# Half of the first modulation on TensorE, one pair's down blocks later, the mixer's gate and loads moved

## The chip, the core and the metric

The kernel runs on one core of a Trainium2 chip. Its time is the device time of one execution in microseconds (us); a kernel's time is the median over its runs. The core has five engines that run side by side and wait for each other by semaphores: PE (TensorE, matmuls; PEld is its weight load), DVE (VectorE), ACT (ScalarE), POOL (GpSimd) and SP (SyncE, which here only issues DMAs). Each engine works through its own list of instructions in order. A DMA that waits for a free buffer therefore holds every DMA behind it in the same list.

## The reference, cut to what matters

One layer of an encoder: x is 1024 rows of 1024 numbers, and three sublayers change it one after the other. `silu(c) @ w_ada + b_ada` gives nine vectors of 1024: a shift, a scale and a gate for each sublayer.

```python
mod = (silu(c) @ w_ada + b_ada).reshape(b, 3, 3, D_MODEL)

def sublayer(h, i, fn, resid_w):
    shift, scale, gate = mod[:, i, 0], mod[:, i, 1], mod[:, i, 2]
    u = rms_norm(h, norm_pre[i]) * (1.0 + scale) + shift
    return h + resid_w * gate * rms_norm(fn(u), norm_post[i])

h = sublayer(h, 0, lambda u: (silu(u @ wg1) * (u @ wu1)) @ wd1, 0.5)
h = sublayer(h, 1, token_mixer, 1.0)
h = sublayer(h, 2, lambda u: (silu(u @ wg2) * (u @ wu2)) @ wd2, 0.5)
```

The hidden width of the two feed-forward networks (FFN) is 2816. The mixer in between projects u to queries, keys, values and two gates, runs two kinds of attention, merges their results by the gates and projects once more. Everything is 32-bit.

## The kernel before, in words

**Matmuls.** Every operand of a large product is split into two fp32r halves, H (a cast on ScalarE) and L (the rest, a subtraction on VectorE), and each product of two tiles is three matmuls: H times H, L times H, H times L. A tile is 128 partitions by 512 columns.

**The FFN, first phase (gate/up).** `ffn` (line 477) runs over eleven pairs of hidden blocks; a pair c has a gate matrix and an up matrix (`Matrix`, line 301). Products of two-by-two blocks are made with seven block products instead of eight (Strassen-Winograd). `start` makes the two products that need plain weights (24 matmuls). `rest` (line 414) makes the other five: `sums` loads the weight blocks again (lines 325 and 327) and forms S2 and S1 on VectorE (lines 330 and 331), `sums34` and `last` make S3, S4 and A22, and then `p6`, `p5`, `p7`, `p3`, `p4` are twelve matmuls each (lines 297 to 299). For the first three pairs (`NFIRST`) `start` has been run ahead of the loop, so only `rest` is left for them.

**Between the two phases.** When a pair is done, `hidden` (line 437) forms the block sums of its result on VectorE (lines 443 to 446) and stores them to DRAM, and `down_sums` (line 462) loads the pair's down weights (lines 465 and 467), forms their sums (lines 470 to 473) and stores them too. For pair 0 both stand at the end of its turn in the loop, in front of pair 1. For a later pair c, `down_sums` stands between its two matrices.

**The FFN, second phase (down).** Seven products p = 0 to 6, each over the eleven pairs: a pair's two blocks are loaded (line 542, tile `stg`, six buffers), split (lines 224 and 225) and multiplied into four PSUM banks, A or B (lines 547 to 549). Product 4 goes on in bank B, whose content after product 3 is first copied out (line 599). The tile `grow` (the sublayer's gate row, line 536) is loaded at the start and used by `finish`. After the last products come post-norm, residual and the next pre-norm.

**The modulation.** Factors that are needed later are formed in small steps by generators. A step is one 512 KB load (line 87) and one multiply-add on VectorE (lines 89 and 91). `mod_col` (lines 97 to 104) turns a vector into columns with eight one-column matmuls (line 101); `mod_gate` makes a gate row in ten steps, with two fp32 matmuls (line 125), loads of the bias and norm rows (lines 119 and 121) and a store (line 130). The gate/up phase takes `per_pair` steps after each pair (3 in the first FFN, 1 in the second), the down phase takes one step at each place in `STEPS`. In the first FFN the gate/up phase makes gate 0 and the factors of sublayer 1 (30 steps), and the down phase makes gate 1 (the mixer's) and the factors of sublayer 2 (30 steps). In the second FFN the gate/up phase makes gate 2 (10 steps).

**The start.** The factors of sublayer 0 are made in `start0_` in four column blocks `cb` of 512 columns, each from four loads of 512 KB (line 654) into eight buffers. VectorE sums eight products into `m0` (lines 658 and 660), and four one-column matmuls against `ones` (line 675) add up the partitions. Lines 679 to 681 finish the factors of two of the eight k-tiles. The transposes of x (line 186), the modulation (lines 177 to 180) and parts of the first `start` products follow, block by block.

**The mixer.** Its first three jobs (queries, keys, values; four weight loads, line 137, into two buffers) are called when the first FFN has been written down in the program.

**Order.** The program is written in one order; a planner at build time then puts each engine's list in order, and may bring an instruction forward where it reckons that its engine is free. `keep_in_program_order` and `issue_after` pin an instruction behind another one.

Of the kernel before, what the change touches and what calls it, by code (L numbers as in the profile page):

```python
# [16 lines left out]
ALU = mybir.AluOpType  # L17
# [21 lines left out]
STEPS = ((0, 2, 4, 6, 8), (0, 2, 4, 6, 8), (2, 4, 6, 8, 10), (2, 6), (0, 4, 8), (4, 6, 8, 9, 10))  # L39
# [7 lines left out]
def build(ctx, tc, A, out):  # L47
# [84 lines left out]
    ab, gates = {}, {}  # L132

# [280 lines left out]
    def rest(late, ms, again):  # L414
# [15 lines left out]
        m.last()  # L430
        m.p6()
# [45 lines left out]
    def ffn(wg, wu, wd, start, pending, steps_fn, per_pair, steps2_fn, i, res_src, dst):  # L477
# [4 lines left out]
        with tc.tile_pool(name="ffa", bufs=1, side="left", reuse_waits="tile") as fp, \  # L482
# [10 lines left out]
            with tc.tile_pool(name="fft", bufs=1, side="left", reuse_waits="tile") as tp, ExitStack() as more:  # L493
# [38 lines left out]
        with tc.tile_pool(name="ffb0", bufs=1, side="left", reuse_waits="tile") as np_, \  # L532
# [3 lines left out]
            SP.dma_start(grow, gates[i])  # L536
# [100 lines left out]
    def start0_(sp, fp, psum, mats):  # L637
# [11 lines left out]
        def matvec(cb):  # L649

            m = sp.tile([P, HALF], F32, name="m0", tag="m0", bufs=3)
            for kq in range(4):
                w = sp.tile([P, 2, HALF], F32, name="w0", tag="row", bufs=8)
                SP.dma_start(w, A["wada0"][cb, kq])
                for i in range(2):
                    cs = csil[:, 2 * kq + i:2 * kq + i + 1]
                    if kq == 0 and i == 0:
                        V.tensor_scalar_mul(m, w[:, i], cs)
                    else:
                        V.scalar_tensor_tensor(m, w[:, i], cs, m, ALU.mult, ALU.add)  # L660
# [3 lines left out]
        for cb in range(4):  # L664
# [8 lines left out]
            ps = psum.tile([P, HALF], F32, name="mps0", tag="y")  # L673
# [626 lines left out]
```

## Time and profile before

| | us |
|---|---|
| median of 3 runs | 2326.88 |
| lowest and highest run | 2324.38, 2332.82 |
| the profiled execution | 2332.79 |
| its span, first to last instruction | 2331.0 |

The table of windows, cut at the kernel's stages, shows where each engine is busy:

| stage | from, to | PE busy | DVE busy | ACT busy | PEclk | DMA share |
|---|---|---|---|---|---|---|
| start | 0, 63 | 33.52 of 63 | 41.09 | 28.41 | 0.85 | 0.70 |
| FFN 1 gate/up | 63, 510 | 433.76 of 447 | 320.40 | 161.19 | 0.98 | 0.52 |
| FFN 1 down | 510, 767 | 236.38 of 257 | 174.35 | 124.48 | 0.95 | 0.79 |
| mixer, attention | 767, 1460 | 668.60 of 693 | 482.33 | 356.37 | 0.99 | 0.17 |
| mixer, merge | 1460, 1640 | 178.06 of 180 | 116.45 | 104.66 | 1.00 | 0.58 |
| FFN 2 gate/up | 1640, 2095 | 439.65 of 455 | 302.78 | 161.56 | 0.98 | 0.45 |
| FFN 2 down | 2095, 2331 | 214.75 of 236 | 133.17 | 110.79 | 0.96 | 0.70 |

PE busy is the sum of its matmuls' times, with overlaps counted once. PEclk is the clock granted to TensorE as a share of the full one; DMA share is the mean busy share of the sixteen DMA engines. A row of the timeline gives the start, the duration, the engine, the line, the operation, the tiles written and read, their shapes and the count; the bracket behind it holds the idle time of the engine before it and what ended that. SPq is SP issuing a DMA: the row's duration is that of the issue, not of the transfer.

### The profile page before, as it was taken

How to read it: one execution, taken by the hardware profiler on the slowest of the kernel's cores; microseconds unless marked ns; L12 is line 12 of the kernel's file. 1: busy time of each engine (PE TensorE's matmuls, PEld its weight loads, DVE VectorE, ACT ScalarE, POOL GpSimd, SP SyncE). 2: the span in 40 equal slices, each digit the busy share in tenths (PEclk: the TensorE clock that was granted, in tenths of full speed). 3: DMA queues.
4: the chain of work that ended last, by engine and by line, in shares of the span. 5: the costliest groups of instructions: out<-in, count | busy, mean ns of one | idle time of the engine just before them, and what ended most of it. 6: DMA issues, size and time to landing. Idle time of an engine off the chain costs nothing.

```text
span 2331.0 us, 28613 instructions
## 1 busy us (share of the span) xinstructions
PE 2204.7 (95%) x10420; PEld 1805.3 (77%) x10420; DVE 1570.6 (67%) x2612; ACT 1047.5 (45%) x1882; POOL 70.0 (3%) x90
## 2 busy tenths in 40 slices
PE   5989999989989989999999999999979999999998
PEld 3767788868868877878888888788767787877876
DVE  6885787566667587576677677665976666655565
ACT  4523333335445465454554455555723332325454
POOL 1000000000000010011001000000000000000000
PEclk8899999999999999999999999999989999999999
DMA  7283574358877211110111122764465443427667
GB/s 298 75 286 131 202 259 175 137 181 304 299 234 237 69 45 40 41 47 29 60 55 64 46 86 87 244 199 128 140 244 179 143 169 138 173 96 261 201 203 246
DMA packets 137678, 364.39 MB, mean 156 GB/s; under 512 B 16704, under 2 KB 20800, under 8 KB 137536
## 3 DMA queue, kind: packets, MB, share of 16 engines
q1 hardware_dynamic: 135904, 356.79, 45.0%
q0 software_dynamic: 1632, 5.77, 0.6%
q8 instruction: 81, 1.33, 0.2%
q14 instruction: 61, 0.50, 0.1%
HBM read 272.32 MB, written 90.18 MB: 156 GB/s over the span
## 4 chain that ended last, share of the span: by engine, by line
PE 67%; DVE 17%; DMA 8%; ACT 4%; issue 3%; SPq 0%; DVEq 0%; ACTq 0%
PE bank L299 9%; PE bank L297 9%; PE bank L298 9%; PE pps L765 4%; PE pps L763 4%; PE pps L767 4%; DMA stg<-in_wd 3%; DVE f L960 2%; PE bankA L547 2%; PE bankA L549 2%; PE bankA L548 2%; DMA stg<-d_T 2%; PE bankB L547 2%; PE bankB L548 2%; PE bankB L549 2%
## 5 line engine op out<-in xcount | busy, mean ns | idle before, releaser
L763 PE MATMUL pps<-uH,wsH 128*128 128x512 f32 x512 | 209.7, 410 | 0.0
L765 PE MATMUL pps<-uL,wsH 128*128 128x512 f32 x512 | 205.4, 401 | 0.0
L767 PE MATMUL pps<-uH,wsL 128*128 128x512 f32 x512 | 204.7, 400 | 0.0
L225 DVE TENSOR_TENSOR tbL<-stg,tbH 128x512 fp32r<-128x512 f32 x154 | 105.8, 689 | 113.7 <-ACT tbH L224 113.4
L224 ACT CAST tbH<-stg 128x512 fp32r<-128x512 f32 x154 | 95.6, 621 | 167.8 <-DMA stg<-d_T 98.6
L547 PE MATMUL bankA<-tbH,sbH 128*128 128x512 f32 x352 | 140.8, 402 | 18.3 <-ACT tbH L224 17.9
L297 PE MATMUL bank<-uH,wsH 128*128 128x512 f32 x352 | 141.4, 404 | 3.5 <-DVE uH L179 2.7
L298 PE MATMUL bank<-uL,wsH 128*128 128x512 f32 x352 | 140.3, 398 | 1.5 <-POOL uL L180 1.5
L548 PE MATMUL bankA<-tbL,sbH 128*128 128x512 f32 x352 | 140.4, 399 | 0.0
L549 PE MATMUL bankA<-tbH,sbL 128*128 128x512 f32 x352 | 139.6, 397 | 0.0
L299 PE MATMUL bank<-uH,wsL 128*128 128x512 f32 x352 | 139.2, 396 | 0.0
L224 ACT CAST wsH<-s 128x1024 fp32r<-128x1024 f32 x88 | 91.6, 1049 | 97.1 <-DVE s L331 88.0
L141 DVE TENSOR_TENSOR wsL<-raw,wsH 128x1024 fp32r<-128x1024 f32 x72 | 87.9, 1221 | 69.1 <-ACT wsH L140 67.5
L225 DVE TENSOR_TENSOR sbL<-stg,sbH 128x512 fp32r<-128x512 f32 (+1 forms) x176 | 108.8, 620 | 36.3 <-ACT sbH L224 34.6
L224 ACT CAST sbH<-stg 128x512 fp32r<-128x512 f32 (+1 forms) x176 | 98.9, 565 | 70.8 <-DMA stg<-hd_A 40.7
L364 ACT COPY q<-bank 128x512 f32<-128x512 f32 x44 | 25.8, 587 | 209.2 <-PE bank L299 209.2
L547 PE MATMUL bankB<-tbH,sbH 128*128 128x512 f32 x264 | 104.5, 396 | 11.3 <-ACT y L599 10.9
L767 PEld LDWEIGHTS pps<-uH,wsL 128*128 128x128 f32 x512 | 96.9, 189 | 17.9
L763 PEld LDWEIGHTS pps<-uH,wsH 128*128 128x128 f32 x512 | 97.6, 191 | 14.7
L225 DVE TENSOR_TENSOR wsL<-s,wsH 128x1024 fp32r<-128x1024 f32 x88 | 106.9, 1218 | 2.6 <-ACT wsH L224 2.0
L765 PEld LDWEIGHTS pps<-uL,wsH 128*128 128x128 f32 x512 | 97.2, 190 | 14.7
L548 PE MATMUL bankB<-tbL,sbH 128*128 128x512 f32 x264 | 104.2, 395 | 0.0
(247 smaller groups left out, 5947.7 us busy)
## 6 DMA issues: line engine op xcount, KB each, us to landing
wada<-in_wada SPq DMA_DIRECT2D x56, 512.0 KB, 5.6
raw<-in_wg SPq DMA_DIRECT2D x50, 512.0 KB, 6.7
raw<-in_wu SPq DMA_DIRECT2D x50, 512.0 KB, 4.4
raw<-in_wd SPq DMA_DIRECT2D x44, 512.0 KB, 4.5
stg<-hd_A SPq DMA_DIRECT2D x88, 256.0 KB, 4.3
stg<-d_S SPq DMA_DIRECT2D x88, 256.0 KB, 3.1
stg<-d_T SPq DMA_DIRECT2D x88, 256.0 KB, 3.5
d_S<-s SPq DMA_DIRECT2D x40, 512.0 KB, 2.7
```

The costliest lines, as they stand in the source:

```text
L141: eng.tensor_sub(l, raw, h.bitcast(F32))
L224: ACT.copy(h, src)
L225: V.tensor_sub(l, src, h.bitcast(F32))
L297: PE.matmul(ps, H[:, ks], bH, start=first and k == 0, stop=False, skip_group_check=not first)
L298: PE.matmul(ps, H[:, ks], bL, start=False, stop=False, skip_group_check=not first)
L299: PE.matmul(ps, L[:, ks], bH, start=False, stop=k == 3, skip_group_check=not first)
L547: PE.matmul(ps, sH[:, ts], tH, start=first, stop=False, skip_group_check=not check)
L548: PE.matmul(ps, sH[:, ts], tL, start=False, stop=False, skip_group_check=not check)
L549: PE.matmul(ps, sL[:, ts], tH, start=False, stop=last, skip_group_check=not check)
L763: PE.matmul(ps, aH, bH, start=i == 0, stop=False)
L765: PE.matmul(ps, aH, bL, start=False, stop=False)
L767: PE.matmul(ps, aL, bH, start=False, stop=i == n - 1)
```

## The change

In `start0_`, column blocks 0 and 1 are no longer summed by VectorE. TensorE multiplies the loaded weights themselves with `silu(c)`: 32 one-column matmuls a block into four PSUM banks. Blocks 2 and 3 stay as they were.

In `ffn`, `hidden` and `down_sums` of pair 0 move from the end of pair 0 into the first matrix of pair 1, behind its sums and in front of its `p6`. `grow` is loaded at the start of product 2 instead of ahead of product 0.

Gate 1 moves from the first FFN's down phase to its gate/up phase (40 steps there, 20 in the down phase). Pair 1 takes 2 steps, pairs 2 to 9 take 5, pair 10 none; `STEPS` is thinned out. In the second FFN pairs 2 to 10 take two steps, pair 1 none.

The mixer's first loads are put behind load number 22 of the first FFN's down phase, the first of product 1.

```diff
-STEPS = ((0, 2, 4, 6, 8), (0, 2, 4, 6, 8), (2, 4, 6, 8, 10), (2, 6), (0, 4, 8), (4, 6, 8, 9, 10))
+STEPS = ((6, 8, 10), (0, 3, 6, 9), (1, 3, 5, 7), (2, 6, 9), (2, 5, 8), (4, 6, 8))
...
-    def rest(late, ms, again):
+    def rest(late, ms, again, between=None):
...
         m.last()
+        if between is not None:
+            between()
         m.p6()
...
+                    def first_blocks():
+                        hidden(late, 0, mats[0][1].c, hd)
+                        down_sums(fp, late, A[wd][0], 0, hd)
+
                     for c in range(NPAIR):
                         if c == 0:
                             rest(late, mats[c], True)
-                        else:
-                            for second, m in enumerate(mats[c] if c < NFIRST else pair(c)):
-                                if second:
-                                    down_sums(fp, late, A[wd][c], c, hd)
-                                m.start()
-                                rest(late, [m], c < NFIRST)
+                            continue
+                        for second, m in enumerate(mats[c] if c < NFIRST else pair(c)):
+                            if second:
+                                down_sums(fp, late, A[wd][c], c, hd)
+                            m.start()
+                            rest(late, [m], c < NFIRST, first_blocks if c == 1 and not second else None)
                         hidden(late, c, mats[c][1].c, hd)
-                        if c == 0:
-                            down_sums(fp, late, A[wd][c], c, hd)
-                            continue
-                        for _ in range(per_pair):
+                        for _ in range(per_pair(c)):
                             next(steps, None)
...
             grow = np_.tile([P, D], F32, name="grow", tag="grow")
-            SP.dma_start(grow, gates[i])
...
+            loads = []
+            after[:] = [loads]
...
-                SP.dma_start(t, A[wd][c][:, B[n]] if n in B else hd[n, c])
+                loads.append(SP.dma_start(t, A[wd][c][:, B[n]] if n in B else hd[n, c]))
...
+                if p == 2:
+                    SP.dma_start(grow, gates[i])
...
-                            if h == 0 and c % 2 == 0:
+                            if h == 0 and c == 0:
                                 next(steps, None)
...
         def matvec(cb):
-            m = sp.tile([P, HALF], F32, name="m0", tag="m0", bufs=3)
+            ws = []
             for kq in range(4):
                 w = sp.tile([P, 2, HALF], F32, name="w0", tag="row", bufs=8)
                 SP.dma_start(w, A["wada0"][cb, kq])
...
+                ws.append(w)
+            if cb < 2:
+                return ws
...
+            if cb < 2:
+                ps = [psum.tile([P, HALF], F32, name="mps0", tag="pa", bufs=6)[:, 0:1] for _ in range(4)]
+                for k in range(NK):
+                    for i in range(4):
+                        p = PE.matmul(ps[i], ms[cb][k // 2][:, k % 2, i * P:(i + 1) * P], csil[:, k:k + 1], start=k == 0, stop=k == NK - 1)
+                        if i == 0 and k == 0 and cb:
+                            tc.keep_in_program_order(p)
...
     def steps1(fp, psum):
         yield from mod_gate(fp, psum, 0, 0.5)
         yield from mods(fp, psum, 1)
+        yield from mod_gate(fp, psum, 1, 1.0)

     def steps1b(fp, psum):
-        yield from mod_gate(fp, psum, 1, 1.0)
         yield from mods(fp, psum, 2)
...
-    pending = ffn("wg1", ..., steps1, 3, steps1b, ...)
+    pending = ffn("wg1", ..., steps1, lambda c: 2 if c == 1 else 5 if c < 10 else 0, steps1b, ...)
...
-    ffn("wg2", ..., lambda fp, psum: mod_gate(fp, psum, 2, 0.5), 1, no_steps, ...)
+    ffn("wg2", ..., lambda fp, psum: mod_gate(fp, psum, 2, 0.5), lambda c: 2 if c > 1 else 0, no_steps, ...)
...
-        for job in first:
-            job.load()
+        with tc.issue_after(n.after[0][2 * NPAIR].ins):
+            for job in first:
+                job.load()
```

More of the change, by code (lines that the diff above doesn't have):

```diff
@@ L132, in build @@
     ab, gates = {}, {}
+    after = []
     def split(src, pool=None, tag="ws", bufs=4, eng=V):
@@ L654, in matvec @@
                 SP.dma_start(w, A["wada0"][cb, kq])
[L655 to L660, printed above, removed]
+                ws.append(w)
+            if cb < 2:
+                return ws
+            m = sp.tile([P, HALF], F32, name="m0", tag="m0", bufs=2)
+            for k in range(NK):
+                w, cs = ws[k // 2][:, k % 2], csil[:, k:k + 1]
+                if k == 0:
+                    V.tensor_scalar_mul(m, w, cs)
+                else:
+                    V.scalar_tensor_tensor(m, w, cs, m, ALU.mult, ALU.add)
             return m
@@ L672, in start0_ @@
                 ms.append(matvec(cb + 1))
-            ps = psum.tile([P, HALF], F32, name="mps0", tag="y")
-            for i in range(4):
-                p = PE.matmul(ps[:, i:i + 1], ms[cb][:, i * P:(i + 1) * P], ones[:, 0:1], start=True, stop=True)
-                if i == 0 and cb:
-                    tc.keep_in_program_order(p)
-            V.tensor_add(bcol[:, ks], ps[:, 0:2], badaT[:, ks])
-            V.tensor_add(acol[:, ks], ps[:, 2:4], badaT[:, NK + 2 * cb:NK + 2 * cb + 2])
+            if cb < 2:
+                ps = [psum.tile([P, HALF], F32, name="mps0", tag="pa", bufs=6)[:, 0:1] for _ in range(4)]
+                for k in range(NK):
+                    for i in range(4):
+                        p = PE.matmul(ps[i], ms[cb][k // 2][:, k % 2, i * P:(i + 1) * P], csil[:, k:k + 1], start=k == 0, stop=k == NK - 1)
+                        if i == 0 and k == 0 and cb:
+                            tc.keep_in_program_order(p)
+            else:
+                ps = psum.tile([P, HALF], F32, name="mps0", tag="y")
+                for i in range(4):
+                    p = PE.matmul(ps[:, i:i + 1], ms[cb][:, i * P:(i + 1) * P], ones[:, 0:1], start=True, stop=True)
+                    if i == 0:
+                        tc.keep_in_program_order(p)
+                ps = [ps[:, i:i + 1] for i in range(4)]
+            for i in range(2):
+                k = 2 * cb + i
+                V.tensor_add(bcol[:, k:k + 1], ps[i], badaT[:, k:k + 1])
+                V.tensor_add(acol[:, k:k + 1], ps[2 + i], badaT[:, NK + k:NK + k + 1])
             V.scalar_tensor_tensor(acol[:, ks], acol[:, ks], 1.0, npreT[:, ks], ALU.add, ALU.mult)
@@ L710, in no_steps @@
         yield
[L712 removed]
+    pending = ffn("wg1", "wu1", "wd1", start0, pending0, steps1, lambda c: 2 if c == 1 else 5 if c < 10 else 0, steps1b, 0, lambda t: A["x"][t * P:(t + 1) * P, :], lambda t: h_dram[0][t])
     pending = mixer(locals())
[L716 removed]
+    ffn("wg2", "wu2", "wd2", start_half, pending, lambda fp, psum: mod_gate(fp, psum, 2, 0.5), lambda c: 2 if c > 1 else 0, no_steps, 2, lambda t: h_dram[1][t],
         lambda t: out[t * P:(t + 1) * P, :])
```

2 lines of the change are left out of this document (removed).

## The prediction

> **What bounds the kernel now.** I read the page first, then TensorE's waits, then the timeline around each long one, and the table by windows for the clock and the matmul count behind it.
>
> ```profile
> span 2331.0 us, 28613 instructions
> ...
> PE 2204.7 (95%) x10420; PEld 1805.3 (77%) x10420; DVE 1570.6 (67%) x2612; ACT 1047.5 (45%) x1882; POOL 70.0 (3%) x90
> ...
> PEclk8899999999999999999999999999989999999999
> ```
> ```profile
> PE bank L297 <- ACT wsH L224: 24.2, 4, 9.4
> PE bankA L547 <- ACT tbH L224: 17.9, 3, 8.7
> PE tps L186 <- ACT y L169: 14.4, 4, 9.8
> PE bankB L547 <- ACT y L599: 10.9, 2, 9.0
> PE mps L675 <- DVE m L660: 7.4, 3, 3.4
> ```
> TensorE is the bound: it is idle 2331.0 - 2204.7 = 126 us of the span. The change doesn't remove matmuls, so it can win only this idle time and the slow matmuls that follow it. The waits (total, times, longest) name the places: the start (L186, L675), the matmuls behind a fresh S2/S1 cast (L297, four times), the entry of the down product (L547 on tbH) and one turn of bank B (L547 on L599). All five lie in what the diff touches.
>
> **Term A, the start.** Two of four column blocks of the modulation leave VectorE (8 products each) for TensorE: 32 matmuls each. An fp32 matmul of one column shows as two records, so 64 records a block; the old route had 8.
>
> ```profile
> 10.21 0.48 DVE L658 TENSOR_SCALAR m<-w,csil 128x512 f32<-128x512 f32 x1
> 18.45 1.87 PE L675 MATMUL mps<-ones,m 128*128 128x1 f32 x8 [2.14 <-DVE m L660]
> 20.61 0.16 DVE L681 SCALAR_TENSOR_TENSOR acol<-acol,npreT 128x2 f32<-128x2 f32 x1
> 28.93 0.40 PE L299 MATMUL bank<-uH,wsL 128*128 128x512 f32 x1
> 32.69 1.30 PE L675 MATMUL mps<-ones,m 128*128 128x1 f32 x8 [3.36 <-DVE m L660]
> 34.28 0.16 DVE L681 SCALAR_TENSOR_TENSOR acol<-acol,npreT 128x2 f32<-128x2 f32 x1
> 45.76 1.03 PE L186 MATMUL tps<-ident,y 128*128 128x128 f32 x8
> 48.68 1.02 PE L675 MATMUL mps<-ones,m 128*128 128x1 f32 x8 [1.88 <-DVE m L660]
> 50.00 0.16 DVE L681 SCALAR_TENSOR_TENSOR acol<-acol,npreT 128x2 f32<-128x2 f32 x1
> 56.82 0.63 PE L299 MATMUL bank<-uH,wsL 128*128 128x512 f32 x1
> 63.11 0.16 DVE L681 SCALAR_TENSOR_TENSOR acol<-acol,npreT 128x2 f32<-128x2 f32 x1
> 391.10 1.68 PE mps L101 x16
> 30.00:40.00 10.00, 6.91 (x24) 5.82 (x25) 7.41 (x13) 3.82 (x7) 2.67 (x2) 0.66 1.02 419
> ```
> A record costs 1.87/8 = 0.234 us on a cold TensorE, 0.163 (32.69) and 0.128 (48.68) between, 1.68/16 = 0.105 in the dense phase. From the last record to the finished factors (end of L681) it takes 0.5 (48.68 + 1.02 to 50.16). Block 0 can start when its first weights are there, which VectorE's first product shows: 10.2. TensorE has done little until then, so I take 0.163, the row behind an idle stretch: ready at 10.2 + 64 x 0.163 + 0.5 = 21.1, no earlier than now (20.77). Then come the transposes and twelve products of pair 0, 20.77 to 29.33 = 8.6 us now. Block 1 is held behind them by its program-order mark. It follows 512-wide matmuls, so 0.128: 21.1 + 8.6 + 8.2 + 0.5 = 38.4, four us later than now (34.44). From there TensorE has 12.4 us of queued work (34.44 to 46.79). Now it then waits for VectorE's block 2; with sixteen products gone from VectorE, and the loads arriving at 419 GB/s whatever the engines do, block 2 is summed before TensorE is through: 38.4 + 12.4 + 1.0 + 0.5 = 52.3. The chain to block 3 is 50.16 to 57.45 = 7.3, then cold records, 1.9, and 0.5: 62.0, against 63.27. **A = 1.3 us gained**: what VectorE gives up, TensorE takes over in series. With every new record at 0.105 the same chain ends at 56.8 (6.5 gained), with 0.234 at 73.4 (10.1 lost); I keep both ends.
>
> The Trainium skill ("TensorE: Matmul & The Clock Gate", Part 1) lets the full clock come after about 3.4 us of sustained activity; block 0 would then run 3.4 us cold and the rest at 0.105, ready at an estimated 19.1 instead of 21.1. Its Part 4 says that transposes don't count as activity; if one-column matmuls don't either, all of block 0 is cold and 25.7 follows. No run here shows a long stream of them, so my value stands between.
>
> **Terms B and C, the first pair's blocks.** `hidden` and `down_sums` of pair 0 put eight VectorE operations in front of the sums of pair 1's first matrix, at a place where no `start` product is left to cover them.
>
> ```profile
> 128.97 0.79 PE L297 MATMUL bank<-T2H,wsH 128*128 128x512 f32 x1 [6.13 <-ACT wsH L224]
> 163.25 0.79 PE L297 MATMUL bank<-T2H,wsH 128*128 128x512 f32 x1 [4.45 <-ACT wsH L224]
> 1711.44 0.69 DVE L330 TENSOR_TENSOR s<-raw 128x512 f32<-128x512 f32 x1 [1.25 <-DMA d_S<-s]
> 1713.98 0.80 PE L297 MATMUL bank<-T2H,wsH 128*128 128x512 f32 x1 [9.40 <-ACT wsH L224]
> 128.90:140.00 11.10, 11.03 (x41) 8.71 (x42) 9.14 (x13) 2.76 (x5) 0.00 (x0) 0.85 0.91 317
> 1713.90:1725.00 11.10, 11.02 (x37) 8.70 (x38) 7.48 (x11) 3.46 (x6) 0.00 (x0) 0.75 0.87 311
> 280.00:300.00 20.00, 20.00 (x88) 16.27 (x87) 18.83 (x23) 8.89 (x12) 0.00 (x0) 1.00 0.92 331
> ```
> A dense 20 us holds 88 matmuls, 0.227 us each. Behind the first wait 41 took 11.1 us where 41 x 0.227 = 9.3 do: the reduced clock costs 1.8 on top of 6.13, 7.9 in all. In the second FFN it is 9.40 + 11.1 - 37 x 0.227 = 12.1. There even the buffer of the sums was the first pair's (L330 waits for the store d_S). With the sums ahead, the casts are done before TensorE arrives. Late next is the same pair's second matrix: its second load needs the buffer that `down_sums` of pair 0 now frees late. Cover is the first matrix's 60 matmuls, 13.6 us; eight operations of 0.69 us as in L330's row, a load and the sums fill nearly all of it. I leave 2 us there each: **B = 6, C = 10.** Bounds: all (7.9, 12.1), or 3 lost each where TensorE's fifth product waits for an addition queued behind the blocks. The turn to pair 2 (4.45) keeps its order and its wait.
>
> **Term D, the entry of the first down product.** In-order SP carries the mixer's first weights there, which wait for weight buffers, and then `grow`, whose place is not free until pair 10 is stored.
>
> ```profile
> 510.06 0.33 SPq L137 DMA_DIRECT2D raw<-in_win  x1
> 517.43 0.33 SPq L536 DMA_DIRECT2D grow<-g_dram  x1
> 517.64 0.80 PE L547 MATMUL bankA<-tbH,sbH 128*128 128x512 f32 x1 [5.72 <-ACT tbH L224]
> 511.92:540.00 28.08, 18.87 (x62) 14.72 (x63) 17.51 (x25) 9.87 (x17) 1.23 (x3) 0.76 0.95 331
> ```
> From the last gate/up work (511.92) to 540 TensorE does 62 matmuls, 14.1 us of work in 28.1: 14 us lost. The change puts the mixer's loads behind the 22 loads of product 0 and `grow` into product 2, where the queue is short of nothing but bandwidth, so the first blocks can be loaded and split under pair 10. What stays is a split into memory that the last products still read, behind the last `hidden`: about 4 us (four sums of 0.69 us in `hidden`, then a cast, a subtraction and a bank copy of about that length each, partly side by side). **D = 10** (bounds: 14 gained; 2 lost if the four mixer loads collide in product 1, where DMA is short too: 0.95 in the window above).
>
> **Term E, the mixer's gate.** Ten steps (eight 512 KB loads among them) leave the down product, where DMA is short, for the gate/up phase.
>
> ```profile
> 654.12 0.42 SPq L87 DMA_DIRECT2D wada<-in_wada  x1
> 655.96 0.58 ACT L599 COPY y<-bankB 128x512 f32<-128x512 f32 x1
> 656.59 0.79 PE L547 MATMUL bankB<-tbH,sbH 128*128 128x512 f32 x1 [8.97 <-ACT y L599]
> 647.50:670.00 22.50, 13.10 (x48) 9.93 (x48) 15.08 (x20) 7.99 (x15) 0.00 (x0) 0.77 0.83 262
> ```
> The bank's copy stands in ScalarE's order behind casts of product 4 that wait for loads, and modulation loads run between those. 48 matmuls, 10.9 us, take 22.5: 11.6 lost. The second FFN has the same code without such loads; its wait is 10.9 - 9.0 = 1.9 (waits above). With 20 steps for 30 the loads should be through by then, but which copy stands behind which cast is the planner's. **E = 7** (0 to 9.7). In the gate/up phase even the stretch that these sums fill most (280 to 300: VectorE 18.83 of 20 us, DMA 0.92) leaves TensorE its 88 matmuls, so two more steps a pair are costed at nothing. Without that cover see the last rival. The gate's own matmuls, its two 512 KB row loads and its store only move.
>
> **Term F, the entry of the second down product.** The last gate step ends at the end of gate/up there, and SP's g_dram store holds all first loads.
>
> ```profile
> 2097.20 0.33 SPq L130 DMA_DIRECT2D g_dram<-grow  x1
> 2103.35 0.80 PE L547 MATMUL bankA<-tbH,sbH 128*128 128x512 f32 x1 [8.71 <-ACT tbH L224]
> 2094.60:2116.00 21.40, 12.70 (x45) 10.02 (x45) 9.98 (x15) 6.89 (x12) 0.99 (x2) 0.76 0.91 304
> ```
> 45 matmuls, 10.2 us, take 21.4: 11.2 lost. Two steps a pair from pair 2 end the gate early and `grow` moves. But here the staging buffers lie on gate/up results, some of them in use until the last `hidden`, so I expect the first loads early and a second wait: **F = 5** (0 to 9).
>
> **How the numbers follow.** 1.3 + 6 + 10 + 10 + 7 + 5 = 39.3 us. The profiled execution took 2332.8 us (span 2331.0), which is the slowest of the runs shown; the median is 5.9 less. 2332.8 - 39.3 = 2293.5, on the median's scale 2288 (2287.6).
>
> Rivals, on that scale:
> - **Forecast**, 28 to 50 us gained, 2277 to 2299: chance 0.53.
> - **Only the orders written out by hand work**: the planner again puts copies and loads badly at the down products; D half, E and F nothing: 1.3 + 6 + 10 + 5 = 22, 2305 (2299 to 2311). For it: L599's place was the planner's. 0.20.
> - **Everything goes**: records at 0.105 and all down waits, 6.5 + 7.9 + 12 + 11 + 9.7 + 7 = 54, 2273 (2265 to 2277). Against: places in memory still in use. 0.08.
> - **The waits change place**: pair 1's second matrix waits as long as its first did, B and C nothing, E and F nothing, D half: 1.3 + 5 = 6 us, 2321 (2311 to 2338); the change then doesn't do what it says. For it: that load is just in time by my count. 0.13.
> - **Slower**: five steps a pair. VectorE is in order; a modulation sum that waits for its load in front of the S2/S1 sums stops TensorE. A load takes 5.6 us (row below); once its delay is above the 24 `start` matmuls' 5.4 us of cover it shows. If all eight pairs 2 to 9 lose 5.6 and 1.8 for the clock, 59 us: 2288 + 59 = 2347. Against: at 280 to 300 such sums crowd VectorE and TensorE still runs full. 0.06.
>
> ```profile
> wada<-in_wada SPq DMA_DIRECT2D x56, 512.0 KB, 5.6
> ```
> The range takes the first two and the third but for its outer end: 2268 to 2311, 0.8 of the chances. A measurement here tells about 0.5%, 12 us, from no change. Faster by more: 0.53 + 0.20 + 0.08 and 0.02 of the fourth = 0.83; within: 0.11; slower: 0.06.
>
> **What would show it.** A: the fourth L681 near 62, 64 records a block. B, C: no wait of L297 on the first matrix of pair 1, 0 to 3 us at the second; 4.45 at pair 2 unchanged. D, F: first stg loads issued before the last gate/up matmul, PE idle under 4 and about 5. E: no L87 load among product 4's first casts, L599 within 2 us. Wrong would be: blocks at 0.234 a record, gaps in pairs 2 to 9, or L599 late again.

## The result, and the profile after

The changed kernel is a little slower: 2341.89 us, median of 6 runs (2339.40 to 2347.16), beside 2328.97 for the kernel before (6 runs, 2324.38 to 2332.82). The ratio is 1.0059, with a 95% interval of 1.0044 to 1.0075. The forecast was 2288, and the range, 2268 to 2311, does not hold it.

The head of the page of the changed kernel:

```profile
span 2340.7 us, 28796 instructions
...
PE 2220.8 (95%) x10532; PEld 1822.2 (78%) x10532; DVE 1561.0 (67%) x2604; ACT 1046.5 (45%) x1882; POOL 71.3 (3%) x90
```

TensorE is busy 16 us longer than before, and its idle time is 2340.7 - 2220.8 = 120 us where it was 126. The change took away 6 us of idle time and added 16 us of busy time. The long waits of TensorE, from the timeline of the changed kernel; L298 is a product of gate/up (L297 before), L553 and L554 the down product (L547), L697 the column sums of the first modulation (L675), L607 the copy of bank B (L599):

```profile
66.07 1.36 PE L697 MATMUL mps<-ones,m 128*128 128x1 f32 x8 [3.86 <-DVE m L672]
162.13 0.80 PE L298 MATMUL bank<-T2H,wsH 128*128 128x512 f32 x1 [7.88 <-ACT wsH L225]
182.34 0.51 PE L298 MATMUL bank<-T2H,wsH 128*128 128x512 f32 x1 [4.18 <-ACT wsH L225]
537.98 0.79 PE L554 MATMUL bankA<-tbL,sbH 128*128 128x512 f32 x1 [2.93 <-DVE tbL L226]
673.79 0.79 PE L553 MATMUL bankB<-tbH,sbH 128*128 128x512 f32 x1 [12.77 <-ACT y L607]
1737.72 0.80 PE L298 MATMUL bank<-T2H,wsH 128*128 128x512 f32 x1 [6.51 <-ACT wsH L225]
1758.55 0.50 PE L298 MATMUL bank<-T2H,wsH 128*128 128x512 f32 x1 [4.17 <-ACT wsH L225]
2113.30 0.80 PE L553 MATMUL bankA<-tbH,sbH 128*128 128x512 f32 x1 [9.18 <-ACT tbH L225]
```

Set beside the prediction's rows: the 6.13 at pair 1's first matrix is gone, and 7.88 stands at its second; 9.40 became 6.51 in the same way; 5.72 became 2.93; 8.97 became 12.77; 8.71 became 9.18. The waits mostly changed place.

Where the time went is read from the lag: how much later the same instruction comes than in the kernel before (for runs x1 and x4 see below). The first row is the end of the fourth L705 (L681 before); every other row is the first record of the last product, the one with operand T4, of the pair or matrix named.

| place (its time in the kernel before) | changed kernel | x1: old start | x4: blocks at pair 0 |
|---|---|---|---|
| fourth factors, end of the start (63) | +18.2 | +0.2 | +18.2 |
| pair 2's first matrix (176) | +19.3 | +3.0 | +19.1 |
| end of gate/up 1 (507) | +24.6 | +9.1 | +24.4 |
| FFN 2, pair 0 (1699) | +12.6 | +0.2 | +15.9 |
| FFN 2, pair 1's first matrix (1728) | +0.5 | -11.9 | +14.9 |
| FFN 2, pair 2's first matrix (1762) | +9.6 | -2.9 | +14.6 |
| end of gate/up 2 (2090) | +11.2 | -0.8 | +16.4 |

The whole loss is there when the start ends, and a part of it is won back later: the two profiled spans differ by 9.7 us. The rows of the start in the changed kernel, TensorE's, VectorE's and SP's, and TensorE's row by windows for block 1 (length; then busy time and count of PE, PEld, DVE, ACT, POOL; granted clock; DMA share; GB/s):

```profile
12.28 3.41 PE L690 MATMUL mps<-csil,w 128*128 128x1 f32 x16
...
23.48 3.41 PE L690 MATMUL mps<-csil,w 128*128 128x1 f32 x16
35.73 10.55 PE L690 MATMUL mps<-csil,w 128*128 128x1 f32 x64
```
```profile
25.65 0.16 DVE L703 TENSOR_TENSOR bcol<-mps,badaT 128x1 f32<-128x1 f32 x1 [11.05 <-PE mps L690]
27.12 0.16 DVE L705 SCALAR_TENSOR_TENSOR acol<-acol,npreT 128x2 f32<-128x2 f32 x1
45.03 0.16 DVE L703 TENSOR_TENSOR bcol<-mps,badaT 128x1 f32<-128x1 f32 x1 [11.43 <-PE mps L690]
46.50 0.16 DVE L705 SCALAR_TENSOR_TENSOR acol<-acol,npreT 128x2 f32<-128x2 f32 x1
57.82 0.48 DVE L670 TENSOR_SCALAR m<-w,csil 128x512 f32<-128x512 f32 x1
67.86 0.16 DVE L705 SCALAR_TENSOR_TENSOR acol<-acol,npreT 128x2 f32<-128x2 f32 x1
81.27 0.16 DVE L705 SCALAR_TENSOR_TENSOR acol<-acol,npreT 128x2 f32<-128x2 f32 x1
```
```profile
18.76 8.49 SPq L662 DMA_DIRECT2D w<-in_wada  x4
```
```profile
DMA to landing us min/median/max: 3.4/7.8/10.4
```
```profile
35.70:46.30 10.60, 10.60 (x66) 10.57 (x65) 0.38 (x3) 0.00 (x0) 0.00 (x0) 0.67 0.50 148
```

Three things are seen. First, a one-column record takes 3.41 / 16 = 0.213 us in block 0 and 10.55 / 64 = 0.165 in block 1, so the two blocks hold TensorE for 25 us. The 0.165 is the price of no record: in the trace the first half of block 1's records come 0.111 us apart, and from 39.3 on they come 0.213 apart, although TensorE is busy without a break; the granted clock is 0.67 in the mean of the two. Second, the 48 records of other work that TensorE has queued behind block 1 took 15.5 us (46.7 to 62.2), where they took 12.35 in the kernel before (34.44 to 46.79); the granted clock was 0.69 there against 0.77, and 1.9 us were idle. Third, VectorE, which gave up the two sums, did not work beside TensorE: it stood idle for 11.05 and 11.43 us in front of additions (L703) that wait for TensorE, with block 2's sum (L670, 57.82) behind them in its order. Block 2's four weight loads had been issued by 27.3, and none of w took longer than 10.4 us to land (the row of landings, from the view of the tile w), so the sum could have begun in the second of these gaps. As it was, TensorE waited 3.86 us for it (66.07), against 1.88 in the kernel before.

### The profile page after: what moved, and what is told of

Read it like the earlier page. It is cut to its first block, busy times and chain, and to the rows that moved or that the text cites. A ratio compares the mean times of both kernels' runs of the same rounds, so it can differ in the third digit from the quotient of the medians.

```text
span 2340.7 us, 28796 instructions
## 1 busy us (share of the span) xinstructions
PE 2220.8 (95%) x10532; PEld 1822.2 (78%) x10532; DVE 1561.0 (67%) x2604; ACT 1046.5 (45%) x1882; POOL 71.3 (3%) x90
## 4 chain that ended last, share of the span: by engine, by line
PE 45%; issue 34%; DVE 13%; DMA 5%; ACT 3%; POOL 0%; SPq 0%; DVEq 0%; ACTq 0%; POOLq 0%
PE bank L300 4%; PE bank L298 4%; PE bank L299 4%; PE pps L789 3%; PE pps L787 3%; PE pps L791 3%; PE bankA L554 2%; PE bankA L553 2%; PE bankA L555 2%; DVE f L984 2%; PE bankB L553 2%; PE bankB L554 2%; PE bankB L555 2%; DMA stg<-d_T 1%; PE vps L787 1%
## 5 line engine op out<-in xcount | busy, mean ns | idle before, releaser
L553 PE MATMUL bankA<-tbH,sbH 128*128 128x512 f32 x352 | 139.2, 395 | 9.5 <-ACT tbH L225 9.2
L298 PE MATMUL bank<-uH,wsH 128*128 128x512 f32 x352 | 143.2, 407 | 3.5 <-DVE uH L180 2.2
L554 PE MATMUL bankA<-tbL,sbH 128*128 128x512 f32 x352 | 138.9, 395 | 2.9 <-DVE tbL L226 2.9
L553 PE MATMUL bankB<-tbH,sbH 128*128 128x512 f32 x264 | 103.8, 393 | 16.0 <-ACT y L607 16.0
L554 PE MATMUL bankB<-tbL,sbH 128*128 128x512 f32 x264 | 103.4, 392 | 0.0
```

The source lines that it names most:

```text
L298: PE.matmul(ps, H[:, ks], bH, start=first and k == 0, stop=False, skip_group_check=not first)
L553: PE.matmul(ps, sH[:, ts], tH, start=first, stop=False, skip_group_check=not check)
L554: PE.matmul(ps, sH[:, ts], tL, start=False, stop=False, skip_group_check=not check)
```

## The experiments

Each run is timed beside the kernel before on its own chip (medians from 2328.9 to 2332.5).

| run | us, median (runs) | ratio to before, 95% interval |
|---|---|---|
| x1 changed, with the old start | 2328.67 (10) | 1.0002, 0.9989 to 1.0016 |
| x2 before, with the new start | 2350.34 (4) | 1.0090, 1.0074 to 1.0106 |
| x3 changed, TensorE kept busy ahead | 2342.73 (4) | 1.0056, 1.0040 to 1.0071 |
| x4 changed, blocks at pair 0's end | 2345.12 (4) | 1.0065, 1.0048 to 1.0083 |
| x5 before, block 0 alone by TensorE | 2340.00 (9) | 1.0038, 1.0024 to 1.0052 |
| x6 x1, mixer's loads in product 5 | 2329.09 (10) | 0.9996, 0.9984 to 1.0007 |
| x7 x1, all blocks behind sums | 2295.07 (4) | 0.9848, 0.9829 to 0.9867 |
| x9 x6 and x7 | 2295.65 (4) | 0.9846, 0.9825 to 0.9866 |
| x10 x9, bank B's copy first | 2288.45 (4) | 0.9819, 0.9803 to 0.9834 |
| x11 x5, block 1's sum first | 2332.70 (10) | 1.0004, 0.9992 to 1.0017 |
| x12 x10, staging elsewhere | 2281.09 (5) | 0.9789, 0.9773 to 0.9805 |
| x13 x12, copy first in FFN 1 alone | 2279.16 (5) | 0.9773, 0.9749 to 0.9797 |

### The start: x1, x2, x3, x5, x11

**x1** is the changed kernel with the start of the kernel before: VectorE sums all four blocks, in three buffers.

```diff
-            if cb < 2:
-                return ws
...
-            m = sp.tile([P, HALF], F32, name="m0", tag="m0", bufs=2)
+            m = sp.tile([P, HALF], F32, name="m0", tag="m0", bufs=3)
```

> The changed kernel with all four column blocks of the first modulation summed by VectorE again. Theory (the new start costs the 18.2 us by which the fourth factors are late, 81.43 against 63.27, and nothing later makes that good): 2342 - 18 = 2324 us, fourth factors again near 63. Rival (the lag is absorbed in waits further on, and the loss lies in the other parts): 2335 us or more.

Measured: 2328.67, 13 us under the changed kernel where 18 were expected. The rest of the change is worth nothing in sum (ratio 1.0002); the start alone takes the changed kernel from there to 2341.9.

**x2** is the other half: the kernel before with the new `matvec` and the new loop over the one-column matmuls, and nothing else of the change.

> The kernel before with only the new start. Theory: 2329 + 18 = 2347 us. Rival (absorbed later): under 2335 us. If both this and the run without the new start move by 18 us, the start is additive to the rest of the change.

Measured: 2350.34, 21 us slower. The lag is 18.2 at the fourth factors and 19.7 at the end: what the start loses, nothing behind it takes up. In the changed kernel the same start costs 13; a part is taken up by waits behind it (8.88 at pair 1's second matrix in x1, 7.88 with the late start), and the rest of the difference was not followed.

**x3** keeps TensorE busy before its first one-column matmul, with nine products that nothing reads:

```diff
+        dz = sp.tile([P, HALF], F32, name="dz", tag="dz")
+        POOL.memset(dz, 1.0)
+        dps = psum.tile([P, HALF], F32, name="dps", tag="pb", bufs=1)
+        for i in range(9):
+            PE.matmul(dps, ones, dz, start=True, stop=True)
```

> The changed kernel with nine extra 512-column matmuls on TensorE ahead of the first weights, whose result nobody reads, so that the clock is up when block 0 begins. Theory 1 (the new start is slow because its one-column matmuls run at the low clock): a record of block 0 falls from 0.213 to about 0.11 us, block 0 is ready some 7 us earlier, and most of that stays: 2335 us. Theory 2 (the loss is the serial order: VectorE's sums of blocks 2 and 3 stand in its list behind factors that TensorE makes, so they begin after 46 us whatever the clock): the fourth factors move by 7 us of the 18 at most, 2335 us or more; the sum of block 2 still begins behind the factors of block 1. If records stay at 0.21, the clock doesn't come up by work of this kind: 2342 us.

Measured: 2342.73. Block 0's rows in its timeline, and one row of its table by windows:

```profile
12.22 1.84 PE L695 MATMUL mps<-csil,w 128*128 128x1 f32 x16
...
16.14 2.54 PE L695 MATMUL mps<-csil,w 128*128 128x1 f32 x16
...
19.00 3.41 PE L695 MATMUL mps<-csil,w 128*128 128x1 f32 x16
...
31.03 10.79 PE L695 MATMUL mps<-csil,w 128*128 128x1 f32 x64
```
```profile
16.10:22.40 6.30, 6.30 (x36) 6.22 (x34) 0.38 (x3) 0.00 (x0) 0.00 (x0) 0.58 1.03 418
```

The first 32 records take 1.84 / 16 = 0.115 us each. Then the clock falls (0.58 is the mean over the row), and from 17.1 on a record takes 0.213 again, although TensorE is busy 6.30 of 6.30 us. A dense stream of one-column matmuls did not hold the clock here, and in block 0 of the changed kernel, with 64 records at 0.213, it did not raise it. Block 0's factors come 4.5 us earlier; the lag at the fourth factors falls from 18.2 to 13.8 us, and the time does not fall at all. So the clock is a part of the loss. How large a part is not shown: in x3 the last 23 records of block 0, and again half of block 1's, still took 0.213. An estimate from the rows above: if the 96 records that take 0.213 in the changed kernel took 0.111, TensorE would need 9.8 us less.

**x5** gives TensorE block 0 alone, in the kernel before:

```diff
-            if cb < 2:
+            if cb < 1:
                 return ws
```

> The kernel before, with block 0 of the first modulation alone summed by TensorE (64 one-column products); blocks 1 to 3 stay with VectorE. Theory (TensorE is slow at one-column products, and what it does not sum, VectorE sums beside it): block 0's factors come as in the changed kernel, 6.7 us late (27.1 for 20.4); block 1's sum is ready by then, so that its wait of 3.4 us in the kernel before goes: the fourth factors are 0 to 4 us late, and the time is 2329 to 2333. Rival (every shift of the first factors is carried through): the fourth factors 6 to 7 us late, 2335 to 2336. Second rival (the 18 us come from block 0 alone, by the weight buffers that it frees late): 2340 and more.

Measured: 2340.00. The theory and its first rival fall; the time is the second rival's, but not its cause, as VectorE's rows show:

```profile
25.67 0.16 DVE L695 TENSOR_TENSOR bcol<-mps,badaT 128x1 f32<-128x1 f32 x1 [11.04 <-PE mps L682]
...
33.54 0.47 DVE L662 TENSOR_SCALAR m<-w,csil 128x512 f32<-128x512 f32 x1
...
71.57 0.16 DVE L697 SCALAR_TENSOR_TENSOR acol<-acol,npreT 128x2 f32<-128x2 f32 x1
```

The fourth factors are 8.5 us late (71.57 for 63.11), not 18. Block 1's sum (L662) starts at 33.54, behind block 0's factors and the first casts and splits. VectorE's 11.04 idle us ahead of them hid nothing.

**x11** is x5 with that one order changed: the additions of block 0 are queued behind the last step of block 1's sum.

```diff
+            with ExitStack() as es:
+                if cb == 0:
+                    es.enter_context(tc.issue_after(last[1].ins))
                 for i in range(2):
...
```

> x5 (block 0 alone by TensorE, 2340.0), with VectorE's sum of block 1 put ahead of block 0's factors in its order; in x5 it stood behind them, after 11 us in which VectorE was idle. Theory (of x5's 8.4 us, 6.7 are TensorE's slow one-column products and the rest is that order, which hid none of the sum of block 1): the wait of 3.7 us in front of block 1's column sums goes, the fourth factors are 2 to 5 us late in place of 8.4, 2333 to 2336. Rival (block 1's weights land too late for the sum to be ahead): 7 us late or more, 2338 and up.

```profile
19.49 0.48 DVE L664 TENSOR_SCALAR m<-w,csil 128x512 f32<-128x512 f32 x1
...
64.48 0.16 DVE L702 SCALAR_TENSOR_TENSOR acol<-acol,npreT 128x2 f32<-128x2 f32 x1
```

Measured: 2332.70, level with the kernel before. The sum now starts at 19.49, while TensorE is at block 0, and the fourth factors are 1.4 us late in place of 8.5, less than the 2 to 5 expected. So for one block the order is worth 7.1 us, and with the better order TensorE's slow records cost the little that is left. That both blocks could be had level in this way was not tried.

### Blocks behind weights: x4, x7

**x4** is the changed kernel with pair 0's blocks back at pair 0's end, as before (the loop over pairs of the kernel before, with the new steps).

> The changed kernel with the first pair's hidden and down_sums back at the end of pair 0, in both FFNs. Theory (the wait only moved from the first to the second matrix of pair 1: from 6.13 and 9.40 to 7.88 and 6.51): by the lag after pair 1 the move cost about 1.5 us in the first FFN and won 2.8 in the second, so 2342 + 1 = 2343 us, same. Rival (the move is worth the 16 us that I forecast and something else hides it): 2355 us or more.

The waits are back at the first matrices in the timeline of x4:

```profile
146.73 0.80 PE L298 MATMUL bank<-T2H,wsH 128*128 128x512 f32 x1 [6.13 <-ACT wsH L225]
...
1729.86 0.80 PE L298 MATMUL bank<-T2H,wsH 128*128 128x512 f32 x1 [9.39 <-ACT wsH L225]
```

Measured: 2345.12. By the table of lags, from the start to pair 2 the first FFN loses 0.9 us with the blocks at pair 0 and 1.1 with them moved; in the second FFN (1699 to 1762, +15.9 to +14.6 against +12.6 to +9.6) the move wins 1.7. By the lag the move itself is worth 1 to 2 us; the times (1.0065 and 1.0059, with overlapping intervals) do not tell the two kernels apart. Why so little is seen in the changed kernel, SP's row and VectorE's in front of the wait at 162.13:

```profile
146.11 5.90 SPq L463 DMA_DIRECT2D d_T<-t  x3
152.06 0.45 SPq L326 DMA_DIRECT2D raw<-in_wu  x1
```
```profile
159.05 0.69 DVE L331 TENSOR_TENSOR s<-raw 128x512 f32<-128x512 f32 x1 [5.60 <-DMA raw<-in_wu]
```

SP issues in order. The second matrix's loads (in_wu) stand behind the stores of d_T, and these wait for VectorE's differences, pair 0's and pair 1's. The load is issued at 152.06, and VectorE then waits 5.60 us for it.

**x7** treats the next three places as the change treated the first: every group of blocks goes behind the sums of a matrix.

```diff
+                            between = None
+                            if c == 1 and not second:
+                                between = first_blocks
+                            elif c in (1, 2) and second:
+                                between = lambda: down_sums(fp, late, A[wd][c], c, hd)
+                            elif c == 2:
+                                between = lambda: hidden(late, 1, mats[1][1].c, hd)
+                            elif second:
                                 down_sums(fp, late, A[wd][c], c, hd)
                             m.start()
-                            rest(late, [m], c < NFIRST, first_blocks if c == 1 and not second else None)
-                        hidden(late, c, mats[c][1].c, hd)
+                            rest(late, [m], c < NFIRST, between)
+                        if c > 1:
+                            hidden(late, c, mats[c][1].c, hd)
```

> The changed kernel with the old start (x1), and the same cure at the next three places: pair 1's weight differences for the down product stand behind the sums of its second matrix, pair 1's hidden blocks behind those of pair 2's first matrix, pair 2's differences behind those of its second. Theory (these waits come from the loads and sums that stand behind the blocks in SP's and VectorE's order): the waits of 8.9 and 4.2 us in the first FFN and of 6.5 and 4.2 us in the second fall to 1 us or less, 18 to 24 us with the reduced clock behind them, and some 4 us are lost again where TensorE's fifth product waits for an addition behind the blocks: 2306 to 2314. Rival (the wait only moves on to the next matrix, as it did from pair 1's first to its second): a wait of 5 to 9 us at pair 2's second or pair 3's first matrix, 2322 to 2329.

Measured: 2295.07, 33.6 us under x1 and 11 under the expected range. None of the four waits is left in either FFN (no wait of L298 on wsH above 1 us). They were 8.88 + 4.19 + 6.50 + 4.17 = 23.7 us in x1. By the lag, x7 gains 16.7 us on x1 at the two places of the first FFN and 15.7 at those of the second, 32.4 together, so 8.7 more came with the four waits. One row by windows of x1, behind the first of them, and one of x7 in gate/up:

```profile
145.85:157.00 11.15, 11.10 (x40) 8.50 (x41) 7.95 (x8) 2.60 (x4) 0.00 (x0) 0.83 0.79 291
```
```profile
128.90:140.00 11.10, 11.10 (x49) 9.01 (x48) 10.61 (x15) 4.80 (x8) 0.00 (x0) 1.00 0.88 340
```

Behind the wait 40 matmuls fill 11.15 us at a granted clock of 0.83; at 0.227 they are 9.1. The wait costs its own length and 2.1 us of slow matmuls, and there were four. The 4 us that I expected to lose at TensorE's fifth product did not show.

### The turn of bank B, and the entries: x6, x9, x10, x12, x13

In the changed kernel the mixer's first loads went to the very place that was to be cleared, SP's and ScalarE's rows before the wait at 673.79:

```profile
643.57 0.43 SPq L138 DMA_DIRECT2D raw<-in_win  x1
...
654.69 0.33 SPq L138 DMA_DIRECT2D raw<-in_wv  x1
```
```profile
647.63 1.05 ACT L141 CAST wsH<-raw 128x1024 fp32r<-128x1024 f32 x1 [1.87 <-DMA raw<-in_win]
...
672.11 0.62 ACT L225 CAST tbH<-stg 128x512 fp32r<-128x512 f32 x1 [2.88 <-DMA stg<-in_wd]
672.64 0.61 ACT L225 CAST sbH<-stg 128x512 fp32r<-128x512 f32 x1
673.16 0.58 ACT L607 COPY y<-bankB 128x512 f32<-128x512 f32 x1
```

**x6** lets them come only behind the first load of product 5, with the old start:

```diff
-        with tc.issue_after(n.after[0][2 * NPAIR].ins):
+        with tc.issue_after(n.after[0][10 * NPAIR].ins):
```

> The changed kernel with the old start (run x1: 2328.7), and the mixer's first four weight loads allowed only behind the first load of product 5, where x1 allows them from product 1 on. Theory (the planner put these loads, their casts and their subtractions right ahead of product 4's first casts and of bank B's copy): the wait of 12.3 us in front of product 4 falls to 2 to 4 us, as in the second FFN (3.2), and 1 to 3 us come back later; 2319 to 2322. Rival (the copy stands behind casts that wait for product 4's own loads): the wait stays at 9 us or more, 2326 to 2330.

```profile
652.10 0.62 ACT L225 CAST tbH<-stg 128x512 fp32r<-128x512 f32 x1 [2.87 <-DMA stg<-in_wd]
...
655.11 0.58 ACT L607 COPY y<-bankB 128x512 f32<-128x512 f32 x1
```
```profile
655.73 0.79 PE L553 MATMUL bankB<-tbH,sbH 128*128 128x512 f32 x1 [9.24 <-ACT y L607]
```

Measured: 2329.09, as x1, and the wait 9.24 for 12.34. The rival's reading was the right one. With neither the gate nor the mixer's loads near, the copy still stands behind casts of product 4, which wait for product 4's own loads. Bank B was ready at 655.73 - 9.24 = 646.5. Little of the 3 us is left in the end: x6 has a wait of 2.71 us at 724.03, in a later product, that x1 does not have, and the medians do not tell the two runs apart.

**x9** joins x6 and x7, with both diffs.

> x6 and x7 together: the old start, the mixer's loads behind product 5's first, and blocks behind sums at all four places. If the two are independent, the gains add: 2328.7 - 8 - 18 = 2303 (2297 to 2310). Rival (the early gate/up phase fills VectorE and DMA, and the entries of the down products take the gain back): 2312 or more.

Measured: 2295.65: the gains add (33.6 and nothing make 33). The wait in front of product 4 was 6.39.

**x10** puts the casts of product 4, from its second pair on, behind the copies:

```diff
-                        s, t = halves(fp, raw(sn, c), "sb", SB), halves(fp, raw(tn, c), "tb", NPAIR)
+                        with ExitStack() as es:
+                            if p == 4 and c:
+                                es.enter_context(tc.issue_after(copies[2].ins))
+                                es.enter_context(tc.issue_after(copies[3].ins))
+                            s, t = halves(fp, raw(sn, c), "sb", SB), halves(fp, raw(tn, c), "tb", NPAIR)
```

> x9 (2295.7), and in both FFNs the casts of product 4 from its second pair on are put behind bank B's copies on ScalarE and VectorE. x6 left a wait of 9.2 us in front of product 4 and x9 6.4, with no modulation and no mixer load near: there the copy stood behind casts of product 4 whose loads came 1.5 to 4 us apart. Theory (it is that order alone): the wait falls to 1 to 3 us in the first FFN and stays at about 2 in the second; with the reduced clock behind it 4 to 6 us gained, 2290 to 2292. Rival (product 4 is short of its own loads, a pair in 2.7 us where TensorE uses one in 2.7): TensorE waits for casts later in product 4 and the time stays at 2294 to 2297.

Measured: 2288.45, 7 us under x9; beside their own kernels before, the two intervals just overlap (0.9819 and 0.9846). The wait is under 1 us in both FFNs, so it was that order. A new one stands in front of product 6 of the second FFN, in x10's waits of TensorE (total, times, longest):

```profile
PE bankA L561 <- DVE y L624: 6.3, 2, 6.0
```

**x12** tests the entry of the second down product. In the changed kernel SP and POOL show this, with SP's longest wait in the window 2080 to 2118 last:

```profile
2073.58 0.42 SPq L548 DMA_DIRECT2D stg<-hd_A  x1
2108.85 0.33 SPq L548 DMA_DIRECT2D stg<-in_wd  x1
```
```profile
2105.71 0.54 POOL L452 DMA_DIRECT2D hd_A<-q  x1
```
```profile
SPq L548 <- DMA hd_A<-q: 34.8, 1, 34.8
```

The first staging load is early. The second is held for 34.8 us, until the store of the last pair's tile q is through; the reading is that its buffer lies on that tile. The run is x10 with the staging buffers 16 KB further on:

```diff
+            if i == 2:
+                pad = np_.tile([P, 4096], F32, name="pad", tag="pad")
```

> x10, and in the second FFN a pad of 16 KB a partition ahead of the staging buffers, so that the first of them no longer lie on the tiles that the last hidden block stores. Theory (the entry of the second down product, 9.2 us in x9, waits for SP's second staging load, which waits for the last store hd_A): that load is issued 6 us earlier or more, the wait falls to 3 to 5 us, 4 to 7 us gained on x10. Rival (the casts then wait for other memory of the last products, or for VectorE): the wait stays at 8 us or more, and the time is x10's within 2 us.

```profile
2031.13 0.33 SPq L558 DMA_DIRECT2D stg<-in_wd  x1
```
```profile
2046.17 0.61 PE L564 MATMUL bankA<-tbL,sbH 128*128 128x512 f32 x1 [2.94 <-DVE tbL L226]
...
2233.51 0.76 PE L563 MATMUL bankA<-tbH,sbH 128*128 128x512 f32 x1 [6.12 <-DVE y L626]
```

Measured: 2281.09. The second load is issued 12 us ahead of the first record of the down product (2042.83), where x10 issued it 5 us behind the last product of gate/up (2048.44 and 2043.30), and the wait is 2.94, what it is in the first FFN. It was the place in memory.

**x13** leaves the second FFN's casts of product 4 to the planner, for the 6.12 in front of product 6:

```diff
-                            if p == 4 and c:
+                            if p == 4 and c and i == 0:
```

> x12 (2281.1), with the casts of product 4 put behind bank B's copies in the first FFN alone. In x10 and x12 a new wait stands in front of product 6 of the second FFN (6.0 and 6.1 us): VectorE's additions of product 5 stand behind subtractions of product 6 that wait for loads. Theory (the pin in the second FFN made the planner write that order; it took away a wait of 2.3 us there and cost 6): the wait in front of product 6 goes, 2 to 3 us come back in front of product 4, and 3 to 5 us are gained on x12, 2276 to 2278. Rival (product 6 is short of its loads whatever the order): the wait stays, and the time is 2281 to 2284.

Measured: 2279.16, 0.9773 of the kernel before (0.9749 to 0.9797). That wait is gone, as the theory had it, and 3.75 us stand in front of product 4, a little more than expected. In time the run can't be told from x12, whose interval overlaps. Either beats both kernels, by some 50 us.

## Why the prediction was wrong

- **A, the step that failed most**: 1.3 us gained was forecast, 18.2 were lost. The prediction's chain has the four finished factors at 21.1, 38.4, 52.3 and 62.0; they came at 27.3, 46.7, 68.0 and 81.4 (ends of L705).
  - Blocks 0 and 1 put it behind by 6.2 and 2.1. The price of a record was 0.163 and 0.128 us, taken from short rows; it was 0.213 and, in the mean, 0.165. That makes 64 x 0.050 = 3.2 and 64 x 0.037 = 2.4 us, and block 0's first record came at 12.28, not at 10.2: 7.7 together. The row to go by was the cold one, 0.234: its end of the range gave 10.1 lost.
  - Block 2 added 7.5. The "12.4 us of queued work" took 15.5, and "with sixteen products gone from VectorE, and the loads arriving at 419 GB/s whatever the engines do, block 2 is summed before TensorE is through" fell: TensorE then waited 3.86 us for that sum. The sentence took idle time of an engine for room to work in. VectorE's order put block 2's sum behind additions that wait for TensorE.
  - Block 3 added 3.7: it took 13.4 us, as in the kernel before (13.1), and the chain had 9.7.
  - So some 11 us are TensorE's own (its late start, the price of a record and the slower work behind block 1), and up to 7.6 are sums that VectorE did not make in time. x5 and x11, alike but for one such order of VectorE, differ by 7.1 us: for one block that order decides whether TensorE's lateness is made up again. For the two blocks of the change this is argued from the rows and was not tested.
- **The Trainium skill** ("TensorE: Matmul & The Clock Gate"): by Part 1, as I applied it, block 0 was to be ready at 19.1 (19.3, with the cold row's 0.234 for the first 3.4 us); by Part 4, if one-column matmuls don't count as activity, at 25.7. Its factors ended at 27.3 (L705), with the first record 2.1 us later than either has it, and the rows of block 1 and of x3 show the clock fall under a full stream of them. Part 4's reading holds here, for an operation that the page does not name.
- **B and C** (6 and 10 forecast): the waits went where the prediction said that they would, to the second matrix, and the size was off: 7.88 and 6.51 where I "left 2 us there each". The count of VectorE's operations in the cover was not the limit; SP's order was, with the loads behind the stores. Measured against x4, -0.2 and 1.7 (in x1, with the old start, the first FFN loses 2.8 up to pair 2). Pair 2's wait kept, as forecast (4.18, 4.17). For B and C this is the fourth rival in its mechanism.
- **D** (10 forecast): right in mechanism and near in size. 5.72 and 3.49 became one wait of 2.93, where I left 4. From the end of gate/up to the first record of product 1 (556 in the kernel before) the lag falls from +24.6 to +13.3 in the changed kernel and from +9.1 to -0.8 in x1. Of this 1.8 is a group of column sums that stood there before (510.08) and comes earlier now; D's own share is 9.5 and 8.
- **E** (7 forecast): wrong in cause. "The loads should be through by then" took modulation loads for what delayed the copy. With the last of them issued at 638.13, some 23 us before bank B was ready, the wait was 12.8, for the mixer's loads had come there, and with those gone too 9.24 (x6). From the first record of product 3 to that of product 5 the lag of the changed kernel grows by 3.0. The copy's place in ScalarE's order was the cause, which the prediction named and did not price; x10 shows it.
- **F** (5 forecast): its reservation was the whole of it. The first load is early, the second waits for a stored tile, and the wait stays at 9.18. The lag falls by 1.4 us up to product 1, no more than the gate's two products that moved away from there (1.9 us at 2092.8 in the kernel before). x12 gives 2.94.
- **Five steps a pair** (the slow rival): no such series of waits; the longest in these pairs is 1.07 us (1.74 in x1). In x1 the lag grows by 6.1 from pair 2 to the end of gate/up, of which 3.7 is work that moved there (the gate's two products and a group of column sums) and 2.4 is not accounted for.

The time fell on the slower side by a mechanism that no rival had as its own; the bound of A (10.1 lost) was on record, but added to the other terms' gains. With A at -18 and only D left of the rest, the sum by the prediction's own steps would have been a loss of 8.

## What to carry to other kernels

Before work is moved from a busy engine to one that is "in series anyway", write down the in-order list that the first engine will have: what it gives up is a gain only if something that can run stands next in its list. A wait cured at one place by putting independent work behind the critical loads comes back at the next place with the same order; treat all of them at once, as x7 did, for 33 us where the first alone was worth 1 or 2. For a wait on a copy or a load, look at what stands ahead of it in that queue, and at whose memory its buffer lies on, before naming the traffic nearby as the cause.

## What the runs showed of the hardware

- TensorE can be busy all the time and lose its clock. Under one-column fp32 products a record went from 0.111 to 0.213 us after 3.6 us in block 1 of the changed kernel (35.73 to 39.3, nothing else between) and after 4.9 us in block 0 of x3 (12.22 to 17.1).
- The clock column can mislead at the head of a trace. For 12.2 to 26.9 us in the changed kernel it reads 1.00, while a record takes 0.213 us. In block 1 the records of 0.111 and those of 0.213 have 0.67 in the mean, so 0.213 does not go with 1.00:

```profile
12.20:26.90 14.70, 14.69 (x71) 14.61 (x70) 0.69 (x5) 3.35 (x5) 0.00 (x0) 1.00 1.03 403
```

- A wait of TensorE of 4 to 9 us cost some 2 us more than its length here: four waits of 23.7 us together were worth 32.4 where they stood (x7 against x1).
